# Normalised rows copied by DMA into one-pass-type tiles and transposed as that type

## The chip, the cores and the metric

The kernel runs on one core of a Trainium2 chip. The metric is the device time of one execution in microseconds, as the median of repeated runs. Profiles are of one execution each, taken by the hardware profiler; their times count from the span's start.

## What is computed

A two-layer encoder in float32 runs over two requests, of 512 and 256 tokens, with shared weights. Width is 1024, the hidden width of the feed-forward blocks 2816. Each layer is

```
x = x + 0.5 * FFN(rmsnorm(x, g0))
x = x + Mixer(rmsnorm(x, g1))
x = x + 0.5 * FFN(rmsnorm(x, g2))

rmsnorm(x, g) = x * rsqrt(mean(x*x) + 1e-6) * g
FFN(h) = (silu(gate) * up) @ w2,   gate, up = split(h @ w1)
```

The mixer of layer 0 is a gated linear recurrence in both directions (HGRN2); that of layer 1 is attention in a window of 128 tokens to each side, with partial rotation and sinks. A last rmsnorm ends it. So there are six normalisations that feed a matmul: before f0, before HGRN, before f1, before f2, before attention, before f3 (f0 to f3 are the four FFNs). The code numbers them by `row`, 0 to 5.

## The kernel before, in words

**Tokens and halves.** The 768 tokens are six blocks of 128 rows, b0 to b5. x lives in SBUF as six tiles of 128 x 1024 with tokens on the partitions. Blocks 0 to 2 are half 0, blocks 3 to 5 half 1; each half has 384 tokens (`H`, `HB = 3`).

**Precision.** Matmuls are float32 products made of three passes of a one-pass type, `float32r`. Every operand is split into a high part (a cast to float32r, on ACT, L166, L199, L265) and a low part (the difference, on DVE, L167, L200, L266), and `mm3` (L258 to L262) issues high x high, high x low, low x high. The FFN's wide products use the seven products of Strassen's scheme (`up_pair` L436, `down_quad` L500).

**Normalising and transposing.** A matmul needs its activations with features on the partitions. When the last contribution to a block of x has been added (L520, L522), `norm_block` runs: ACT squares the row and sums it (L310), ACT takes the root (L311), DVE the reciprocal (L312), and DVE multiplies x by it into a new tile `xn` (L313). `turn(half, part, row)` then transposes on TensorE: for each of four groups of 128 features it makes three transposes, one for each block of the half, side by side in one PSUM tile (L330), and ACT moves the tile out with the gain g as its scale (L341, or L344 with DVE's low part L345 in front of a mixer; L337 and L338 in the first one). A turn of half 0, part 0 makes features 0 to 511 for b0, b1, b2. Per row that is 2 halves x 2 parts x 4 groups x 3 blocks = 48 transposes, 288 in all. They are issued as plain float32, with the identity read as float32.

In attention, tiles that are float32r already are transposed as that type by `transpose_r` (L931), and its probabilities as float32 (L1167).

**Order.** Everything is traced in program order, and a planner then orders each engine's instructions by their readiness as it expects it, with program order as the priority; semaphores enforce the dependences. Within one engine instructions run strictly in the order so written. `later` and `run_later` put the turns off: a block's end calls `after_block` (L381), which queues the two turns of a half when its third block is done; `run_later` runs one queued step after b4, one after b5, and the rest among the first matmuls of the next stage. So, in program order, half 0's turns stand behind the matmuls of b4 and of b5 and half 1's among the first products of the next FFN (`up_plain`) or the first projection of the mixer (`proj_tok`).

**Queues.** Weights are loaded by DMAs issued from SP (L151, L185) and combined by accumulating DMAs from GpSimd (L141). ACT issues the DMAs that spill x around each mixer (L591) and bring it back (L597), and the small tables. A DMA issue that waits for a semaphore stands in its engine's order like any other instruction.

**Tiles.** `big` is a pool of 21 slots of 128 x 6 KB. `xn`, the transposed operands (14 in use through an FFN) and the hidden activations come from it.

The change touches `load_x` (L282 to L285), `norm_block` (L304) and `turn` (L317), and adds two helpers.

Of the kernel before, what the change touches and what calls it, by code (L numbers as in the profile page):

```python
# [9 lines left out]
F32 = mybir.dt.float32  # L10
F32R = mybir.dt.float32r
# [5 lines left out]
P = 128  # L17
# [18 lines left out]
HB = H // P  # L36
# [11 lines left out]
class Trunk:  # L48
# [219 lines left out]
    def load_x(self, srcs):  # L268
        nc = self.nc
        self.x = [None] * NBLK  # L270
        last = None
        blocks = [srcs[s][lo : lo + P, :] for s, (_, n) in enumerate(SEQS) for lo in range(0, n, P)]
        for b, src in enumerate(blocks):
            self.x[b] = self.xt()
            with self.tc.issue_after(last) if last else nullcontext():
                last = nc.sync.dma_start(self.x[b], src).ins
            if b == HB - 1:
                with self.tc.issue_after(last):
                    self.load_next()
                    self.load_next()  # L280
                last = self.last_load.ins
        order = None  # L282
        for b in range(HB):
            with self.tc.issue_after(order) if order else nullcontext():
                order = self.norm_block(b, vector=b == 1) or order  # L285
        self.turn(0, 0, 0, True)
        self.turn(0, 1, 0, True)
        with self.tc.issue_after(order):
            self.stage_next()
            self.stage_next()  # L290
        self.load_tables()

        def rest():
            for b in range(HB, NBLK):
                self.norm_block(b)
            for part in range(2):
                for kp in range(2):
                    self.block(part, 0, 0)
                    o = self.ops[(f"b{part}0", kp)].bitcast(F32)
                    nc.vector.tensor_add(self.tn[(part, 0)][:, kp], o[:, :, 0, :], o[:, :, 1, :])  # L300

        self.later(rest, lambda: self.turn(1, 0, 0), lambda: self.turn(1, 1, 0), self.sums)

    def norm_block(self, b, vector=False):  # L304
        nc = self.nc
        xn, r = self.big([P, D]), self.stat(1)
        if vector:
            nc.vector.tensor_tensor_reduce(xn, self.x[b], self.x[b], 1.0, 0.0, ALU.mult, ALU.add, r)
        else:
            nc.scalar.activation(xn, self.x[b], AF.Square, accum_out=r)  # L310
        last = nc.scalar.activation(r, r, AF.Sqrt, bias=self.eps, scale=1.0 / D).ins  # L311
        nc.vector.reciprocal(r, r)  # L312
        nc.vector.tensor_scalar(xn, self.x[b], r, None, ALU.mult)  # L313
        self.xn[b] = xn
        return last

    def turn(self, half, part, row, first=False):  # L317
        nc = self.nc
        feeds_ffn = row % 3 != 1
        if half == 0 and part == 0:  # L320
            if feeds_ffn:
                self.ops = {}
                self.tn = {}
            else:
                self.h = [self.big([P, 2, T], F32R) for _ in range(NC)]
        for m in range(4 * part, 4 * part + 4):
            pt = self.ps(H)
            for i in range(HB):
                src = self.xn[HB * half + i][:, m * P : (m + 1) * P]
                nc.tensor.transpose(pt[:, i * P : (i + 1) * P], src, self.ident)  # L330
            g = self.cols[:, row * NC + m : row * NC + m + 1]
            if first:
                name, kp = f"b{part}{half}", m % 4 // 2
                if (name, kp) not in self.ops:
                    self.ops[(name, kp)] = self.big([P, 2, 2, H], F32R)
                hi, lo = self.operand(name, m % 4)
                nc.scalar.activation(hi, pt, AF.Copy, scale=g)  # L337
                nc.vector.scalar_tensor_tensor(lo, pt, g, hi.bitcast(F32), ALU.mult, ALU.subtract)  # L338
                continue
            if feeds_ffn:  # L340
                nc.scalar.activation(self.block(part, half, m % 4), pt, AF.Copy, scale=g)  # L341
                continue
            hi, lo = (self.h[m][:, i, half * H : (half + 1) * H] for i in range(2))
            nc.scalar.activation(hi, pt, AF.Copy, scale=g)  # L344
            nc.vector.scalar_tensor_tensor(lo, pt, g, hi.bitcast(F32), ALU.mult, ALU.subtract)  # L345
        if feeds_ffn and not first:
            for kp in range(2):
                self.put(f"b{part}{half}", kp, self.tn[(part, half)][:, kp])
# [30 lines left out]
    xn = [None] * NBLK  # L379
# [925 lines left out]
```

## Time and profile before

| | |
|---|---|
| median of 3 runs | 2813.54 us (2812.93 to 2815.74) |
| span of the profiled execution | 2810.8 us |
| TensorE busy | 2781.0 us, 99% |
| TensorE weight loads | 2557.5 us, 91% |
| DVE busy | 2171.4 us, 77% |
| ACT busy | 1321.2 us, 47% |
| GpSimd busy | 372.5 us, 13% |
| granted TensorE clock, mean | 0.999 |
| moved by DMA | 291.37 MB, mean 104 GB/s |

The profiled execution's own time is its span, 2.7 us below the median of the runs.

How to read the rows: L330 is line 330 of the kernel. PE is TensorE's matmul (transposes too), PEld its weight load, DVE VectorE, ACT ScalarE, POOL GpSimd, SP SyncE; a name with q is that engine's sequencer. In a timeline a row is: start in us, duration in us, engine, line, operation, out<-in by the names of tiles, shapes, xcount of merged instructions, and in brackets the idle time before it and what ended it. In the groups of instructions, behind the bar, stand total busy us and the mean ns of one, then the idle time before. Matmuls are pipelined: the duration of one (0.27 us for a transposition) is longer than the distance from one to the next, and the distance is what a stream of them costs. The chain is followed back from the last instruction to what released each step; only what is on it sets the end.

### The profile page before, as it was taken

Reading aid. Unit: us, or ns where it says so; the run is one execution under the profiler, and the core shown is the slowest. Engines: PE = TensorE matmul, PEld = TensorE weight load, DVE = VectorE, ACT = ScalarE, POOL = GpSimd, SP = SyncE. Lnnn points to the kernel's source line nnn. Section 1 sums busy time; section 2 is a strip of 40 time slices with the busy share of each in tenths; the row PEclk is TensorE's granted clock in tenths of the full one; section 3 lists DMA queues with packets and bytes.
Section 4 is the critical chain, followed back from the end, with each engine's and each line's share of the span. In section 5 each row is a group of like instructions: output and inputs, shape, how many; then the busy total and the mean of one; then the engine's idle time right before and its main releaser. Section 6 shows DMA issues by size and latency. Waiting matters only on the chain.

```text
span 2810.8 us, 40561 instructions
## 1 busy us (share of the span) xinstructions
PE 2781.0 (99%) x15225; PEld 2557.5 (91%) x15225; DVE 2171.4 (77%) x3760; ACT 1321.2 (47%) x2447; POOL 372.5 (13%) x402
## 2 busy tenths in 40 slices
PE   8999999999999999999999999999999899999998
PEld 8999999889899889999999999999888789999998
DVE  8788788477577558878878887887848878878877
ACT  7444444434344336444444644444457756444443
POOL 2111120000000001111111111111102211211110
PEclk9999999999999999999999999999999999999999
DMA  6554464311111133555454355545422013555543
GB/s 174 127 128 120 113 147 123 106 44 38 46 38 38 61 98 76 136 132 126 117 129 120 76 142 132 124 116 124 135 72 76 33 50 83 143 134 125 119 114 108
DMA packets 330100, 291.37 MB, mean 104 GB/s; under 512 B 11608, under 2 KB 257840, under 8 KB 329904
## 3 DMA queue, kind: packets, MB, share of 16 engines
q1 hardware_dynamic: 293920, 212.37, 26.0%
q0 software_dynamic: 31680, 62.93, 13.0%
q10 hardware_dynamic: 4304, 13.49, 1.4%
q8 instruction: 119, 1.95, 0.3%
q14 instruction: 77, 0.63, 0.1%
HBM read 216.39 MB, written 9.44 MB: 80 GB/s over the span
## 4 chain that ended last, share of the span: by engine, by line
PE 95%; ACT 2%; DVE 2%; POOL 0%; issue 0%; DMA 0%; ACTq 0%; DVEq 0%; POOLq 0%
PE ps L436 41%; PE ps L500 20%; PE ps L262 8%; PE ps L260 8%; PE ps L261 8%; PE ps L692 3%; PE ps L786 1%; PE ps L330 1%; PE ps L762 1%; ACT big L1145 1%; PE ps L1167 1%; POOL big L1161 0%; PE ps L1129 0%; PE ps L931 0%; DVE x L522 0%
## 5 line engine op out<-in xcount | busy, mean ns | idle before, releaser
L436 PE MATMUL ps<-big,w 128*128 128x384 f32 x6720 | 1169.3, 334 | 0.0
L436 PEld LDWEIGHTS ps<-big,w 128*128 128x128 f32 x6720 | 1165.9, 188 | 1.7 <-ACT tA L453 0.2
L199 ACT CAST w<-wr 128x512 fp32r<-128x512 f32 x600 | 416.2, 707 | 687.2 <-PE ps L436 277.8
L500 PE MATMUL ps<-w,big 128*128 128x512 f32 x2520 | 575.3, 389 | 0.0
L500 PEld LDWEIGHTS ps<-w,big 128*128 128x128 f32 x2520 | 472.7, 188 | 97.5
L200 DVE TENSOR_TENSOR w<-wr,w 128x512 fp32r<-128x512 f32 (+1 forms) x520 | 434.7, 840 | 146.6 <-ACT w L199 130.8
L522 DVE SCALAR_TENSOR_TENSOR x<-ps,x 128x512 f32<-128x512 f32 x468 | 301.8, 682 | 10.0 <-PE ps L262 9.9
L141 POOL DMA_DIRECT2D s<-wr x120 | 105.9, 882 | 1511.1 <-DMA wr<-in_ffn_w_dram 643.0
L260 PE MATMUL ps<-w,big 128*128 128x512 f32 x624 | 249.3, 400 | 0.3
L262 PE MATMUL ps<-w,big 128*128 128x512 f32 x624 | 244.8, 392 | 2.1 <-DVE big L1005 1.1
L261 PE MATMUL ps<-w,big 128*128 128x512 f32 x624 | 244.0, 391 | 0.0
L260 PE MATMUL ps<-big,w 128*128 128x384 f32 (+2 forms) x640 | 220.4, 346 | 0.5 <-ACT w L166 0.4
L261 PE MATMUL ps<-big,w 128*128 128x384 f32 (+2 forms) x640 | 216.2, 338 | 0.2
L262 PE MATMUL ps<-big,w 128*128 128x384 f32 (+2 forms) x640 | 215.3, 336 | 0.0
L265 ACT CAST big<-tA 128x384 fp32r<-128x384 f32 x296 | 148.0, 513 | 114.0 <-DVE tA L475 36.2
L167 DVE TENSOR_TENSOR w<-wr,w 128x1024 fp32r<-128x1024 f32 x92 | 111.8, 1221 | 83.9 <-ACT w L166 78.5
L266 DVE TENSOR_TENSOR big<-tA,big 128x384 fp32r<-128x384 f32 x296 | 164.7, 567 | 6.7 <-ACT big L265 4.5
L200 POOL TENSOR_TENSOR w<-wr,w 128x512 fp32r<-128x512 f32 x80 | 135.4, 1692 | 202.6 <-ACT w L199 202.6
L166 ACT CAST w<-wr 128x1024 fp32r<-128x1024 f32 x92 | 96.6, 1052 | 122.2 <-PE ps L261 100.6
L206 DVE TENSOR_TENSOR wr<-wr,wr 128x512 f32<-128x512 f32 (+1 forms) x120 | 127.1, 1059 | 21.8 <-issue 20.8
L262 PEld LDWEIGHTS ps<-w,big 128*128 128x128 f32 x624 | 117.1, 188 | 28.5 <-DVE big L1005 1.9
L141 POOL DMA_DIRECT2D wr<-wr x100 | 88.1, 881 | 405.0 <-DVE w L200 166.5
(174 smaller groups left out, 3279.1 us busy)
## 6 DMA issues: line engine op xcount, KB each, us to landing
wr<-in_ffn_w_dram SPq DMA_DIRECT2D x264, 512.0 KB, 4.0
s<-in_ffn_w_dram SPq DMA_DIRECT2D x120, 256.0 KB, 3.2
s<-wr POOLq DMA_DIRECT2D x120, 256.0 KB, 4.9
wr<-wr POOLq DMA_DIRECT2D x80, 256.0 KB, 3.8
wr<-in_hg_w_in_dram SPq DMA_DIRECT2D x40, 512.0 KB, 3.8
wr<-wr POOLq DMA_DIRECT2D x20, 512.0 KB, 4.6
spill<-x ACTq DMA_DIRECT2D x12, 512.0 KB, 3.1
x<-spill ACTq DMA_DIRECT2D x12, 512.0 KB, 3.3
```

Of the source, the lines that this page charges most:

```text
L141: self.nc.gpsimd.dma_start(out, src, accum_op=ALU.add)
L199: nc.scalar.copy(h, src)
L200: (eng or nc.vector).tensor_sub(l, src, h.bitcast(F32))
L206: add = {"second": lambda: nc.vector.tensor_add(a11, a11, a21), "fourth": lambda: nc.vector.tensor_add(a12, a12, a11)}
L260: nc.tensor.matmul(out, a[0], b[0], start=first, stop=False)
L261: nc.tensor.matmul(out, a[0], b[1], start=False, stop=False)
L262: nc.tensor.matmul(out, a[1], b[0], start=False, stop=last)
L265: self.nc.scalar.copy(hi, src)
L266: self.nc.vector.tensor_sub(lo, src, hi.bitcast(F32))
L436: self.nc.tensor.matmul(ps, a[x], b[y], start=first and k == 0 and i == 0, stop=k == 3 and i == 2, skip_group_check=True,)
L500: nc.tensor.matmul(ps, a[x], w[y], start=name == chain and kp == 0 and q == 0, stop=kp == 1 and q == 2, skip_group_check=True,)
L522: self.nc.vector.scalar_tensor_tensor(x, ps, c, x, ALU.mult, ALU.add)
```

## The change

Outside the first half of the first normalisation, the normalised rows of the first two blocks of each half (b0, b1, b3, b4) are copied, byte for byte, by a DMA that ACT issues, into a new tile declared float32r, and the transposes of these blocks are issued in that type with the float32r identity (`transpose_r`). The third block of each half (b2, b5) is transposed as float32 as before. DMA writes the bits unchanged, where a cast to float32r would round them.

```diff
-                order = self.norm_block(b, vector=b == 1) or order
+                order = self.norm_block(b, vector=b == 1, first=True) or order
...
-    def norm_block(self, b, vector=False):
+    def norm_block(self, b, vector=False, first=False):
...
         nc.vector.tensor_scalar(xn, self.x[b], r, None, ALU.mult)
-        self.xn[b] = xn
+        self.xn[b] = xn if first or b % HB == HB - 1 else self.raw_copy(xn)
         return last
+
+    def raw_copy(self, src):
+        t = self.big(src.shape, F32R)
+        self.nc.scalar.dma_start(t.bitcast(F32), src)
+        return t
+
+    def turn_over(self, dst, src):
+        if src.dtype == F32R:
+            self.transpose_r(dst, src)
+        else:
+            self.nc.tensor.transpose(dst, src, self.ident)
...
-                nc.tensor.transpose(pt[:, i * P : (i + 1) * P], src, self.ident)
+                self.turn_over(pt[:, i * P : (i + 1) * P], src)
```

In numbers: 22 copies of 512 KB (two before f0, four before each of the other five), and 176 of the 288 transposes in the other type. Nothing else is changed.

## The prediction

> **What bounds the kernel now.** I read the page first (busy shares, then the chain that ended last), then that chain in order of time at the six places where L330 transposes, then the timelines of PE, DVE and ACT there.
>
> ```profile
> span 2810.8 us, 40561 instructions
> ...
> PE 2781.0 (99%) x15225; PEld 2557.5 (91%) x15225; DVE 2171.4 (77%) x3760; ACT 1321.2 (47%) x2447; POOL 372.5 (13%) x402
> ...
> PE 95%; ACT 2%; DVE 2%; POOL 0%; issue 0%; DMA 0%; ACTq 0%; DVEq 0%; POOLq 0%
> ...
> L330 PE MATMUL ps<-ident_r,big 128*128 128x128 f32 x288 | 41.0, 285 | 1.2 <-DVE big L313 1.2
> ```
>
> TensorE is busy 99% of the span and holds 95% of the chain, so at first sight each nanosecond taken from a transposition is a nanosecond of the kernel. The last row limits the prize: the L330 transposes are 288 instructions and 41 us of busy time. The 24 of half 0 at the start are left as they are; of the other 264 two in three change type, 176.
>
> Whether a saved nanosecond counts is a matter of the stage. The chain by line, and a few of its pieces in order of time (start, us, what):
>
> ```profile
> by line: PE ps L436 41.5%; PE ps L500 20.4%; PE ps L262 8.3%; PE ps L260 8.3%; PE ps L261 8.3%; PE ps L692 3.3%; PE ps L786 0.9%; PE ps L330 0.6%; PE ps L762 0.6%; ACT big L1145 0.5%; PE ps L1167 0.5%; POOL big L1161 0.4%; PE ps L1129 0.3%;
> ...
> 8.86 2.63 PE ps L330 x11
> ...
> 499.64 1.31 PE ps L330 x12
> ...
> 1540.18 1.32 DVE big L313 x2
> ...
> 1542.90 1.15 ACT big L310 x2
> ...
> 1544.70 1.41 ACT big L341 x3
> ...
> 2052.32 0.63 PE ps L931 x8
> ```
>
> L330 has 0.6% of the chain: 0.006 x 2810.8 = 16.9 us. The 2.63 us at 8.86 are unchanged ones. That leaves 14.3 us, at 1.31 / 12 = 109 ns each about 130 of the 264 on the chain. Around the others the chain runs through DVE and ACT: in the stage between the first two FFNs that follow each other (1540 to 1546), through the normalising multiply L313, the squares L310 and the evictions L341. A faster transposition there frees nobody.
>
> **What a transposition saves.** The chain rows give 109 ns for a float32 one and 0.63 / 8 = 79 ns for one of the one-pass type (L931, attention). The changed groups are mixed, two of the new type and then one old, and for that the nearest rows are those where attention has both side by side:
>
> ```profile
> 2143.75 0.46 PE L931 MATMUL ps<-ident_r,big 128*128 128x128 f32 x4
> 2144.05 0.62 PE L1167 MATMUL ps<-ident_r,big 128*128 128x128 f32 x4
> ...
> 2230.82 0.54 PE L931 MATMUL ps<-ident_r,big 128*128 128x128 f32 x4
> 2231.19 0.62 PE L1167 MATMUL ps<-ident_r,big 128*128 128x128 f32 x4
> ```
>
> Start to start, four take 0.30 us behind matmuls (75 ns each) and 0.37 us right behind float32 ones (93 ns each). So one saves 16 to 34 ns; I take 25. On the chain, 130 x 2/3 = 87 of them: **2.2 us** (1.4 to 3.0). If all 176 counted: 4.4 us (2.8 to 6.0).
>
> A rule speaks against this. The Trainium skill, "TensorE: Matmul & The Clock Gate", section "LDWEIGHTS (loading the stationary operand)", has a weight load cost columns / 1.2 ns, an estimate of 107 ns here for either type, since each transposition loads a new stationary block. By it 109 ns could fall by 2 and the saving would be about nothing; the 75 to 79 ns above say that loads follow each other faster than that, but no row shows the exact mixture.
>
> **What the copies add.** There are 22 (b3 and b4 for the first FFN, then four per stage for five stages), each 512 KB, from SBUF to SBUF, issued by ACT behind the DVE multiply. No such copy is in the trace. The nearest rows are the spills, also 512 KB and also issued by ACT:
>
> ```profile
> L591 ACTq DMA_DIRECT2D spill<-x x12: 326/333/1642, 491.0 to 2046.2; - x12
> ...
> DMA to landing us min/median/max: 2.6/3.1/5.8
> ```
>
> I take 3.1 us from issue to landing, with 2.6 and 5.8 as ends. A block used to be ready when L313 ended; now it is ready 3.1 us later. Is there room? For half 0 the late one is b1 (b0 is earlier and b2 isn't copied). Its L313 and the first transposes, for the stages before the HGRN mixer, f2, attention, and f1:
>
> ```profile
> 497.75 0.75 DVE L313 TENSOR_SCALAR big<-x,stat 128x1024 f32<-128x1024 f32 x1
> ...
> 499.47 1.48 PE L330 MATMUL ps<-ident_r,big 128*128 128x128 f32 x12
> ...
> 1540.10 1.41 DVE L313 TENSOR_SCALAR big<-x,stat 128x1024 f32<-128x1024 f32 x2
> ...
> 1541.98 1.47 PE L330 MATMUL ps<-ident_r,big 128*128 128x128 f32 x12
> ...
> 2030.21 0.75 DVE L313 TENSOR_SCALAR big<-x,stat 128x1024 f32<-128x1024 f32 x1
> ...
> 2031.94 0.27 PE L330 MATMUL ps<-ident_r,big 128*128 128x128 f32 x1
> ...
> 1046.52 0.75 DVE L313 TENSOR_SCALAR big<-x,stat 128x1024 f32<-128x1024 f32 x1
> ...
> 1052.05 0.49 PE L330 MATMUL ps<-ident_r,big 128*128 128x128 f32 x3
> ```
>
> Before the HGRN mixer b1 is ready at 498.50, its copy at 501.6, the transposes begin at 499.47: **2.1 us late**. Before f2: 1540.80 + 3.1 = 1543.9 against 1541.98, 1.9 late. Before attention: 2030.96 + 3.1 = 2034.1 against 2031.94, 2.1 late. Before f1, where blocks come out of the output projection, 1047.27 + 3.1 = 1050.4 against 1052.05: in time, by 1.7. The stage before f3 has the same shape as f1's. So three stages out of five have a copy that is late by about 2 us, 1.4 at the short end (2.6 us, before f2) and 4.8 at the long end (5.8 us).
>
> What happens then depends on the order in which PE's instructions were written. That this order follows readiness and not the program shows where half 1 is transposed:
>
> ```profile
> 508.20 0.71 PE L330 MATMUL ps<-ident_r,big 128*128 128x128 f32 x5
> 508.67 0.48 PE L261 MATMUL ps<-w,big 128*128 128x512 f32 x1
> 508.98 0.27 PE L330 MATMUL ps<-ident_r,big 128*128 128x128 f32 x1
> ```
>
> The program issues the transposes of half 1 three by three, b3, b4, b5. Here they come five, then singly between matmuls of the projection: each was set where its block was expected. I therefore expect b5's twelve matmuls to be moved ahead of b1's transposes. At the spacing of
>
> ```profile
> 1543.52 0.40 PE L261 MATMUL ps<-w,big 128*128 128x512 f32 x1
> 1543.75 0.40 PE L262 MATMUL ps<-w,big 128*128 128x512 f32 x1
> ```
>
> 0.23 us they last 2.8 us, which covers the 2 us. It isn't free before f2, where the chain goes on through ACT's evictions:
>
> ```profile
> 1542.90 1.06 ACT L310 ACTIVATE big<-x 128x1024 f32<-128x1024 f32 x1 [1.21 <-DVE x L522]
> ...
> 1543.96 0.56 ACT L341 ACTIVATE big<-ps,cols 128x384 f32<-128x384 f32 x1
> ```
>
> The first eviction needs all three blocks of a tile. With b1 landing at 1543.9, a transposition and its 0.27 us behind it, it starts at about 1544.4 and not 1543.96: **0.4 us**. Before the two mixers the chain runs on through DVE, and b5's additions (L522), which come 1.3 us earlier when PE takes b5 first, are what it follows; I charge **0.3 us** for each, with 0 and 2 as ends.
>
> For half 1, b3 and b4 have more room. Before f2 the rows are:
>
> ```profile
> 1545.44 0.76 DVE L313 TENSOR_SCALAR big<-x,stat 128x1024 f32<-128x1024 f32 x1
> ...
> 1547.73 0.60 PE L330 MATMUL ps<-ident_r,big 128*128 128x128 f32 x4
> ```
>
> The multiply is b4's; its copy is there at 1549.3. The four transposes are b3's alone, b4's come later, among the matmuls of the first projection. I cost half 1 at nothing; those matmuls are its cover, and without them each late copy would cost its lateness.
>
> **At the start** there is less room:
>
> ```profile
> 19.75 1.41 DVE L313 TENSOR_SCALAR big<-x,stat 128x1024 f32<-128x1024 f32 x2
> ...
> 22.29 1.04 PE L330 MATMUL ps<-ident_r,big 128*128 128x128 f32 x8
> ...
> 24.23 0.44 PE L260 MATMUL ps<-big,w 128*128 128x384 f32 x1 [0.39 <-ACT w L166]
> ...
> 21.65 1.28 ACT L311 ACT_TABLE_LOAD   x1
> ```
>
> The eight transposes at 22.29 fill time in which PE would wait for ACT's cast (it still waits at 24.23). Their copies land at about 24.2, so they move to where PE is the bound: 8 x 85 ns = **0.7 us**. If ACT's order shifts here, a table load more or less is 1.3 us; so 0 to 2.
>
> **On ACT** a DMA issue waits for its L313 and everything behind it on ACT (squares, casts, evictions) waits too, at most L312 and L313, about 0.9 us. ACT idles before squares for longer than that (1.21 us in the row above), and issues that do not wait cost it nothing visible. I charge **0.5 us** over the kernel; the ends are 0 and 3. The Trainium skill, "Perfetto Trace Analysis", section "DMA Instruction — HWDGE (DVE, Sync)", puts such a wait in the sequencer, so that nothing behind it is even queued; no row here has a waiting issue on ACT. DVE gets no work. The copies are 22 x 0.52 = 11.5 MB, and the two extra tiles per half come when the FFN's 14 operand tiles are free: nothing for either, and if a weight load is pushed back by a copy, up to the copy's 3.1 us, its staging has slack in these stages.
>
> **Sum:** -2.2 + 0.4 + 0.6 + 0.7 + 0.5 = 0.0 us. The profiled span stays 2810.8 and the median, 2.7 us above it, stays at **2813.5**. A measurement of this kernel can tell about 0.2%, 5.6 us, from no change.
>
> **The rivals.**
> *The order keeps b1's transposes in front* (slower). PE then stands still until the copy lands: 1.9 us before f2, and before the two mixers, where spills sit in the same ACT queue, between 2.1 (landing 3.1) and 4.8 (landing 5.8), say 3.5 each. 8.9 - 2.2 + 0.7 + 0.5 = +7.9: **2821.5**, from 2818 to 2824. For it: the expected landing by which the order is written need not be the real one. Against it: the scattered transposes above. It decides once PE's wait in front of L330 exceeds about 2.5 us per stage.
> *Everything counts* (faster). The DVE and ACT chains have slack that the chain view hides, all 176 save 34 ns and the order costs nothing: -6.0, **2807.5**. Against it: the pieces at 1540 to 1546, which hold no PE.
> *The new type isn't quicker in this mixture*, because the weight load sets the pace at 109 ns for both: 0 + 2.2 of costs, **2815.7**. Against it: 75 to 93 ns next to float32 ones. The LDWEIGHTS rule above would have it so.
>
> **Chances.** Forecast 0.53, order kept 0.30, everything counts 0.12, not quicker 0.05. Faster by over 0.2%: 0.10 (most of the third); slower by over 0.2%: 0.25 (most of the second, a little of the first); the rest, 0.65, within. The range, 2807.0 to 2823.0, holds the forecast, the fourth case, half of the third and most of the second.
>
> **What would show it.** Right: L330 split into about 176 and 112, the former 75 to 93 ns apart; copies landing 2.6 to 3.5 us after issue; before f2 and the mixers b5's L260 to L262 standing ahead of b1's transposes; PE's wait in front of L330 under 1 us per stage. Wrong: PE waits of 2 us and more on a copy; ACT idle behind its own DMA issues by over 3 us in all; a change in the FFN loops (52 to 480 and the like), which I expect to be equal to the microsecond.

## The result and the profile after

The change made the kernel slower: **2863.66 us** (2861.92 to 2864.51, 4 runs) against 2814.58 us (2812.93 to 2815.74, the three runs above and a fourth), a ratio of 1.0178 (1.0166 to 1.019). The forecast was 2813.5 with a range up to 2823.0. The profiled execution has a span of 2861.5 us, 50.7 more than that of before. In the kernel after, the multiply is still L313; the copy is L319, the float32 transposes L326, those of the one-pass type L942 (attention's 144 among them), the evictions L352 and L355 with the low part L356, the additions to x L531 and L533.

The page of the kernel after, its span, busy times and chain:

```profile
span 2861.5 us, 40606 instructions
...
PE 2791.4 (98%) x15225; PEld 2564.9 (90%) x15225; DVE 2165.9 (76%) x3760; ACT 1326.4 (46%) x2449; POOL 370.1 (13%) x402
...
PE 93%; DVE 3%; ACT 3%; DMA 1%; issue 0%; POOL 0%; ACTq 0%; DVEq 0%; POOLq 0%
```

TensorE stands idle for 2861.5 - 2791.4 = 70.1 us, against 2810.8 - 2781.0 = 29.8 before: **40.3 of the 50.7 us are new idle time**. The other 10.4 are busy time, though 176 transposes became cheaper. What TensorE waited for (total us, times, longest):

```profile
PE ps L260 <- ACT big L265: 19.2, 3, 7.3
PE ps L260 <- DVE big L356: 12.6, 2, 6.3
...
PE ps L942 <- DMA big<-big: 4.3, 4, 3.0
PE ps L326 <- DVE big L313: 3.5, 3, 1.8
```

The two large rows are five waits of about 6 to 7 us, one in each of the five stages between two blocks of the network, and TensorE waits there for the operands of the next stage: the split (L265) of an eviction in front of an FFN, the low part (L356) in front of a mixer. For the copies themselves it waits 4.3 us, 3.0 of them in one wait at the start. The same view for ScalarE:

```profile
ACT big L310 <- DVE big L313: 23.8, 14, 2.6
...
ACT big L352 <- DVE big L313: 7.5, 3, 2.6
...
ACT big L355 <- DVE big L313: 4.9, 2, 2.5
```

None of the three is in the kernel before. A square does not read what L313 writes, nor does an eviction read the L313 named here; between them and L313 stands a copy's issue. 23.8 + 7.5 + 4.9 = **36.2 us** of ScalarE. The timeline in front of the HGRN mixer shows it, first before (the idle time and what ended it are in the brackets):

```profile
491.02 1.06 ACT L310 ACTIVATE big<-x 128x1024 f32<-128x1024 f32 x1 [0.28 <-DVE x L522]
...
493.69 1.04 ACT L310 ACTIVATE big<-x 128x1024 f32<-128x1024 f32 x1
...
494.95 1.06 ACT L310 ACTIVATE big<-x 128x1024 f32<-128x1024 f32 x1
...
497.67 1.06 ACT L310 ACTIVATE big<-x 128x1024 f32<-128x1024 f32 x1 [1.20 <-DVE x L522]
...
500.59 1.06 ACT L310 ACTIVATE big<-x 128x1024 f32<-128x1024 f32 x1 [1.44 <-DVE x L522]
...
501.65 0.56 ACT L344 ACTIVATE big<-ps,cols 128x384 fp32r<-128x384 f32 x1
```

and after:

```profile
500.76 1.06 ACT L310 ACTIVATE big<-x 128x1024 f32<-128x1024 f32 x1 [0.28 <-DVE x L533]
...
505.55 0.48 ACTq L319 DMA_DIRECT2D big<-big  x1
506.08 1.07 ACT L310 ACTIVATE big<-x 128x1024 f32<-128x1024 f32 x1 [2.56 <-DVE big L313]
...
510.99 0.47 ACTq L319 DMA_DIRECT2D big<-big  x1
511.51 1.06 ACT L310 ACTIVATE big<-x 128x1024 f32<-128x1024 f32 x1 [3.96 <-DMA spill<-x]
...
515.77 0.47 ACTq L319 DMA_DIRECT2D big<-big  x1
516.29 1.06 ACT L310 ACTIVATE big<-x 128x1024 f32<-128x1024 f32 x1 [1.27 <-DVE big L313]
...
520.52 0.47 ACTq L319 DMA_DIRECT2D big<-big  x1
521.04 2.00 ACT L355 ACTIVATE big<-ps,cols 128x384 fp32r<-128x384 f32 x4 [2.47 <-DVE big L313]
```

Before, the squares follow the arrival of the blocks, 1 to 3 us apart. After, each copied block goes through square, root, reciprocal, multiply and issue before the next square starts, 5.3 and 5.4 us apart for the first two. (The 3.96 us in front of the square at 511.51 are put down to a spill, but that square too starts 0.52 us behind the start of a copy's issue; the 36.2 us don't hold this wait.) From the first square to the first eviction it was 501.65 - 491.02 = 10.6 us; now it is 521.04 - 500.76 = **20.3 us**. That is the number to follow through the experiments. It stands for one transition of five: it tells the ends of the range apart, but it doesn't rank the runs between (13.2 and 15.4 us go with nearly the same time).

**The second price is the clock.** Windows of the kernel after around the wait in front of f1 (from:to, length, busy time of PE, PEld, DVE, ACT, POOL with instructions, granted clock, DMA share, GB/s):

```profile
1074.00:1080.00 6.00, 0.11 (x1) 0.00 (x0) 3.41 (x6) 3.35 (x8) 0.87 (x1) 0.67 0.92 279
1080.00:1085.50 5.50, 5.42 (x17) 5.14 (x18) 4.31 (x6) 5.48 (x12) 0.86 (x1) 0.50 0.57 110
1085.50:1095.00 9.50, 9.50 (x65) 9.40 (x64) 3.25 (x5) 6.86 (x13) 0.00 (x0) 0.96 0.00 0
```

TensorE does nothing for 6 us, and for the 5.5 us that follow it runs at a clock of 0.50: 17 instructions in 5.42 us of busy time, where the next window has 65 instructions in 9.50. So this wait of 6 us costs some 2.7 us more (half of 5.5), and that is booked as busy time. In the 10 us behind each of the five waits the mean clock was 0.79, 0.69, 0.76, 0.81 and 0.78, so some 4 to 6 us of each ran at half, an estimate of 11.7 us lost in all. With 2.8 us at the start (below) that is 14.5 us, about what busy time lost: it rose by 10.4 us, though the transposes became some 4.6 us cheaper (the run with the new type alone, below). The Trainium skill, "TensorE: Matmul & The Clock Gate", section "Part 1: The HAM clock gate", has the clock fall to half after an idle window of about 3.4 us and come back after as long a busy one; this trace agrees in kind, with 6 us idle and about 5.5 us at half, but the wait of 3.01 us at the start was followed by half the clock too. The mean granted clock of the span fell from 0.999 to 0.990.

What did not change: the FFN loops. The same stretch of 336 matmuls after and before, from the chains in order of time:

```profile
119.11 58.26 PE ps L447 x336
```

```profile
109.38 58.26 PE ps L436 x336
```

It starts 119.11 - 109.38 = 9.7 us later: a fifth of the 50.7 us is lost ahead of it, around the first normalisation, and the rest between there and the start of f3's loop.

### The profile page after: what moved, and what is told of

It reads as the page before. It is cut to its first block, busy times and chain, and to the rows that moved or that the text cites. A ratio compares the mean times of both kernels' runs of the same rounds, so it can differ in the third digit from the quotient of the medians.

```text
span 2861.5 us, 40606 instructions
## 1 busy us (share of the span) xinstructions
PE 2791.4 (98%) x15225; PEld 2564.9 (90%) x15225; DVE 2165.9 (76%) x3760; ACT 1326.4 (46%) x2449; POOL 370.1 (13%) x402
## 3 DMA queue, kind: packets, MB, share of 16 engines
q0 software_dynamic: 31680, 62.93, 13.2%
## 4 chain that ended last, share of the span: by engine, by line
PE 93%; DVE 3%; ACT 3%; DMA 1%; issue 0%; POOL 0%; ACTq 0%; DVEq 0%; POOLq 0%
PE ps L447 40%; PE ps L511 20%; PE ps L260 8%; PE ps L261 8%; PE ps L262 8%; PE ps L703 3%; PE ps L797 1%; PE ps L942 1%; PE ps L773 1%; PE ps L1178 1%; ACT big L1156 0%; DVE w L167 0%; PE ps L1140 0%; DVE big L313 0%; PE ps L1191 0%
## 5 line engine op out<-in xcount | busy, mean ns | idle before, releaser
L447 PEld LDWEIGHTS ps<-big,w 128*128 128x128 f32 x6720 | 1165.9, 188 | 2.2 <-DVE tA L473 0.6
L511 PEld LDWEIGHTS ps<-w,big 128*128 128x128 f32 x2520 | 472.5, 188 | 100.1 <-ACT big L265 2.5
L533 DVE SCALAR_TENSOR_TENSOR x<-ps,x 128x512 f32<-128x512 f32 x468 | 302.3, 685 | 12.1 <-PE ps L262 12.1
L260 PE MATMUL ps<-big,w 128*128 128x384 f32 (+2 forms) x640 | 224.4, 352 | 19.2 <-ACT big L265 19.2
L261 PE MATMUL ps<-big,w 128*128 128x384 f32 (+2 forms) x640 | 219.7, 344 | 0.0
L262 PE MATMUL ps<-big,w 128*128 128x384 f32 (+2 forms) x640 | 218.1, 341 | 0.0
L265 ACT CAST big<-tA 128x384 fp32r<-128x384 f32 x296 | 148.7, 516 | 118.0 <-DVE tA L479 38.0
L260 PEld LDWEIGHTS ps<-w,big 128*128 128x128 f32 x624 | 118.8, 190 | 35.1 <-DVE big L356 13.1
L260 PEld LDWEIGHTS ps<-big,w 128*128 128x128 f32 x640 | 123.9, 194 | 26.3 <-ACT big L265 19.8
L262 PEld LDWEIGHTS ps<-w,big 128*128 128x128 f32 x624 | 118.3, 190 | 26.9 <-DVE big L1016 1.9
```

Of the source, the lines that this page charges most:

```text
L260: nc.tensor.matmul(out, a[0], b[0], start=first, stop=False)
L261: nc.tensor.matmul(out, a[0], b[1], start=False, stop=False)
L262: nc.tensor.matmul(out, a[1], b[0], start=False, stop=last)
L265: self.nc.scalar.copy(hi, src)
L447: self.nc.tensor.matmul(ps, a[x], b[y], start=first and k == 0 and i == 0, stop=k == 3 and i == 2, skip_group_check=True,)
L511: nc.tensor.matmul(ps, a[x], w[y], start=name == chain and kp == 0 and q == 0, stop=kp == 1 and q == 2, skip_group_check=True,)
```

## The experiments

The kernel before took 2813.08, 2812.61, 2812.74, 2813.18 and 2812.89 us beside the five groups of runs; ratios are to those, with 95% intervals. "Lag" is the time from the first square to the first eviction in front of the HGRN mixer.

| run | median us | ratio | lag us |
|---|---|---|---|
| before | 2814.58 | | 10.6 |
| after | 2863.66 | 1.0178 (1.0166 to 1.019) | 20.3 |
| copies unread | 2860.96 | 1.017 (1.0155 to 1.0186) | 20.3 |
| copies of x | 2821.77 | 1.0031 (1.002 to 1.0042) | 10.9 |
| copies by GpSimd | 2839.02 | 1.0091 (1.0076 to 1.0106) | 15.7 |
| rounded, second tile | 2832.75 | 1.0068 (1.0053 to 1.0083) | 14.5 |
| second tile alone | 2830.23 | 1.0064 (1.0049 to 1.0079) | 14.6 |
| rounded, one tile | 2811.87 | 0.9998 (0.9988 to 1.0007) | 10.6 |
| copy behind next square | 2831.68 | 1.0067 (1.0052 to 1.0082) | 13.2 |
| copies of b0, b1 | 2831.51 | 1.0063 (1.0048 to 1.0078) | 15.4 |
| copies of b3, b4 | 2853.41 | 1.0144 (1.0129 to 1.0159) | 17.0 |
| second tile early | 2814.32 | 1.0005 (0.9996 to 1.0014) | 10.7 |
| copies, tile early | 2828.84 | 1.0059 (1.0047 to 1.0072) | 11.7 |

**First theories.** A: ScalarE, whose instructions run in order, stands behind each copy's issue while that waits for L313. B: the transposes wait for the copies to land. C: the new order of TensorE's instructions, or the new type, costs.

*Copies that nobody reads.*

```diff
-        self.xn[b] = xn if first or b % HB == HB - 1 else self.raw_copy(xn)
+        self.xn[b] = xn
+        if not first and b % HB < HB - 1:
+            self.raw_copy(xn)
```

> The 22 copies are issued by ACT as in the change, but nothing reads them: all transposes read the float32 rows. Theory A (ACT's in-order queue stands behind each copy's issue, which waits for DVE's L313, and the evictions and casts behind it are late): slow nearly as the change, 2845 to 2865 us, with ACT idle for 2 us and more behind single issues. Theory B (the transposes wait for the copy to land, 3.3 us after issue): nothing waits for a copy any more, so 2812 to 2818 us. Theory C (the planner's new order of PE's instructions is itself bad): 2812 to 2820 us, since PE's instructions have the old operands.

2860.96 us. All but 2.7 us of the loss is there with float32 transposes that wait for no copy, and the waits of TensorE are those of the change:

```profile
PE ps L260 <- ACT big L265: 19.0, 3, 7.2
PE ps L260 <- DVE big L358: 12.6, 2, 6.3
```

So B and C don't have the bulk.

*Copies of x in place of the normalised rows* (the issue doesn't wait for L313; what is transposed is then x itself, without the normalisation).

```diff
-        self.xn[b] = xn if first or b % HB == HB - 1 else self.raw_copy(xn)
+        self.xn[b] = xn if first or b % HB == HB - 1 else self.raw_copy(self.x[b])
```

> The copies read x, which is long complete for ACT when its squares are done, and not the normalised rows; so the transposed rows are not normalised. Size, queue, landing and type of the transposes stay, the wait for L313 goes. Theory A: most of the 49 us come back, 2810 to 2822 us. Theory B: the copies start about 1 to 2 us earlier and the transposes still wait for them, 2840 to 2860 us. Theory C: the order is like that of the change, 2850 to 2865 us.

2821.77 us: 41.9 of the 49 us are gone with the wait for L313, though copies, landings and new type are all there. At this point A looked settled.

*Copies issued by GpSimd.*

```diff
-        self.nc.scalar.dma_start(t.bitcast(F32), src)
+        self.nc.gpsimd.dma_start(t.bitcast(F32), src)
```

> The copies are issued by GpSimd and not by ACT; GpSimd is busy 13% of the span. Theory A: ACT has no waiting issue, so 2808 to 2822 us; what is left shows how much the late landing costs. Theory B: landing is no earlier (the 512 KB accumulating copies of GpSimd took 4.6 us), so 2855 to 2875 us. Theory C: 2850 to 2865 us.

2839.02 us. ScalarE has no copy to wait behind, and half of the loss stays. TensorE's wait for copies is larger here, from this kernel's waits:

```profile
PE ps L942 <- DMA big<-big: 12.9, 7, 4.0
```

That explains a part, but the lag is still 15.7 us.

*No copies: L313 writes rounded rows into a second tile of the one-pass type.*

```diff
-        nc.vector.tensor_scalar(xn, self.x[b], r, None, ALU.mult)
-        self.xn[b] = xn if first or b % HB == HB - 1 else self.raw_copy(xn)
+        if first or b % HB == HB - 1:
+            nc.vector.tensor_scalar(xn, self.x[b], r, None, ALU.mult)
+        else:
+            xn = self.big([P, D], F32R)
+            nc.vector.tensor_scalar(xn, self.x[b], r, None, ALU.mult)
+        self.xn[b] = xn
```

> No copies at all: DVE's L313 writes its result directly into a float32r tile for the same blocks, which rounds these rows, and 176 transposes run in that type. This measures what the other type is worth alone. My estimate on record: 2.2 us on the chain, up to 6.0 if all count, so 2808 to 2813 us. All theories expect the same; if the mixture isn't quicker, 2814 to 2815 us.

2832.75 us, the surprise: no DMA, no wait of ScalarE, and yet 19.7 us. A is not enough. What this kernel shares with the change is the new type and the second tile.

*The second tile without the new type, and the new type without a second tile*, to tell theory S (the second tile costs) from theory T (the new type disturbs).

```diff
+        if not (first or b % HB == HB - 1):
+            xn = self.big([P, D])
         nc.vector.tensor_scalar(xn, self.x[b], r, None, ALU.mult)
-        self.xn[b] = xn if first or b % HB == HB - 1 else self.raw_copy(xn)
+        self.xn[b] = xn
```

> No copies and no new type: the only thing left of the change is its second tile per copied block (Square writes into one tile, L313 writes the normalised rows into another, both plain float32). The rounded kernel, which has the second tile and the new type but no copies, lost 18 to 20 us. Theory S (the second tile, taken from a pool of 21, makes squares or allocations late): 2828 to 2836, as much as the rounded kernel and 2 more for the slower transposition. Theory T (the new type itself disturbs): 2811 to 2816. Theory A alone (everything comes from the queue behind the copies): 2811 to 2816 too, so a time near before would leave T for the rounded kernel.

```diff
-        xn, r = self.big([P, D]), self.stat(1)
+        xn, r = self.big([P, D], F32 if first or b % HB == HB - 1 else F32R), self.stat(1)
...
-        self.xn[b] = xn if first or b % HB == HB - 1 else self.raw_copy(xn)
+        self.xn[b] = xn
```

> The new type with no second tile and no copy: the tile of a copied block is a one-pass tile from the start, Square writes its scratch into it and L313 overwrites it with the rounded rows (so the low bits are lost, the transposes are of the new type). Theory S: nothing is left but the quicker transposes, 2808 to 2813 (the sum of the prediction had -2.2 us for them). Theory T: 2828 to 2836, as the rounded kernel with its second tile.

2830.23 and 2811.87 us. The second tile alone costs **17.6 us**; its first square and its first eviction in front of the HGRN mixer are 14.6 us apart:

```profile
495.14 1.06 ACT L310 ACTIVATE big<-x 128x1024 f32<-128x1024 f32 x1 [0.28 <-DVE x L535]
...
509.70 1.96 ACT L357 ACTIVATE big<-ps,cols 128x384 fp32r<-128x384 f32 x4
```

The new type alone can't be told from nothing. The page of the kernel with the type alone:

```profile
span 2810.2 us, 40565 instructions
...
PE 2776.4 (99%) x15225; PEld 2552.0 (91%) x15225; DVE 2166.3 (77%) x3760; ACT 1321.6 (47%) x2447; POOL 375.3 (13%) x402
```

Busy time fell by 2781.0 - 2776.4 = 4.6 us, 26 ns for each of the 176 transposes, and idle time rose from 29.8 to 33.8: what the transposes save is given back as waiting.

*Each copy behind the next block's square; copies of one half only.*

```diff
-            nc.scalar.activation(xn, self.x[b], AF.Square, accum_out=r)
+            square = nc.scalar.activation(xn, self.x[b], AF.Square, accum_out=r).ins
+            if self.uncopied:
+                was, src = self.uncopied.pop()
+                with self.tc.issue_after(square):
+                    self.xn[was] = self.raw_copy(src)
...
-        self.xn[b] = xn if first or b % HB == HB - 1 else self.raw_copy(xn)
+        self.xn[b] = xn
+        if not first and b % HB < HB - 1:
+            self.uncopied.append((b, xn))
```

> All copies, issued by ScalarE, but each one ordered behind the Square of the next block, by when L313 of its own block has had about as long as a Square takes. Theory A (ACT stands behind an issue that waits for L313): the wait shrinks from 2.6 us to under 1, and what remains is the second tile's price: 2820 to 2838. Theory B (the transposes wait for the landing): the copies land later still, 2863 or more. If it is still 2855 or more with short waits of ACT, neither has the cause.

2831.68 us: with the squares freed, 32 us come back and about 19 stay, about as much as the second tile alone costs.

```diff
-        self.xn[b] = xn if first or b % HB == HB - 1 else self.raw_copy(xn)
+        self.xn[b] = xn if first or b % HB == HB - 1 or b > HB - 1 else self.raw_copy(xn)
```

> Copies of blocks 0 and 1 only; blocks 3 and 4 stay plain float32. The prediction held that the second half costs nothing, so that all of the loss would sit in the first half: then 2855 to 2866. If blocks 3 and 4 have a share (their squares and multiplications stand in ACT's and DVE's queues behind the copies of blocks 0 and 1, ahead of f1, attention and HGRN), the loss falls with the number of issues: half of 49 us, 2835 to 2842.

The other half, `b < HB` in that place:

> Copies of blocks 3 and 4 only. The prediction charged the second half at nothing: 2811 to 2816. With the first half alone at 2831.5 and the whole at 2863.7, what is left for the second half, if the two add, is 31 us: 2838 to 2848. In between: the halves do not add, the loss being made where both crowd the same queue and pool.

2831.51 and 2853.41 us. The second half alone costs 40.7 us, twice the first half's 18.9, and the two do not add up to the whole: neither forecast of the second half held.

**Why a tile costs time.** Theory S: a second tile of the pool of 21 crowds it. Rival O: the planner writes another order as soon as the square and L313 don't share a tile. Two tests of S:

```diff
-SLOTS = 21
+SLOTS = 20
```

> The kernel before with nothing changed but the pool: 20 slots in place of 21. Theory S: the pool is short at the transitions, so one slot less costs there too, some 3 to 20 us: 2816 to 2833. Rival O: the number of slots does not matter, 2811 to 2815.

```diff
-        xn, r = self.big([P, D]), self.stat(1)
+        own = first or b % HB == HB - 1
+        xn = self.big([P, D]) if own else self.tp.tile([P, D], mybir.dt.bfloat16, tag="tA", name=self.name("tA"), bufs=8)
+        r = self.stat(1)
...
+        if not own:
+            xn = self.big([P, D])
         nc.vector.tensor_scalar(xn, self.x[b], r, None, ALU.mult)
...
```

> No copies, no new type. As the kernel with the second plain tile per copied block (2830), but Square writes its scratch as bfloat16 into a 2 KB tile of another pool (tA), and the only tile of the pool of 21 is the one that L313 writes. Theory S (the second tile's slot in the pool of 21 is what costs 18 us): 2809 to 2816. Rival O (the planner orders the block otherwise as soon as Square and L313 don't share a tile, slots or not): 2826 to 2834.

One slot less, in the kernel before, costs 4.7 us (2817.46, ratio 1.0017, 1.0007 to 1.0026). With the square's scratch out of the pool, a block holds one tile as before, and still 13.8 of the 17.6 us stay (2826.5, 1.0049, 1.0034 to 1.0064). S falls. The two remedies together, scratch elsewhere and copies behind the next square:

```diff
+        xn = self.big([P, D]) if own else self.tp.tile([P, D], mybir.dt.bfloat16, tag="tA", name=self.name("tA"), bufs=8)
...
+                with self.tc.issue_after(square):
+                    self.xn[was] = self.raw_copy(src)
...
```

> All copies, with both suspects taken down: each copy is issued by ScalarE behind the Square of the next block (no wait for L313), and Square's scratch is a bfloat16 tile of another pool, so that a copied block holds no tile of the pool of 21 before L313 and two only from L313 to the landing of its copy. If A and S are the whole cause: 2812 to 2822, the upper end if two tiles for some 5 us still crowd the pool or if b1's and b4's copies land late. If it stays at 2828 or more, a part of the late copies' 2831.7 has another cause (the landing, or the second tile after L313).

2831.26 us (1.0068, 1.0051 to 1.0085): nothing gained over the late copies alone.

**Theory P**, from the order in which ScalarE's instructions are written: a tile of the pool is handed out in program order of first writers. An instruction that takes a new tile can't be placed ahead of one that stands earlier in the program and takes a tile too. In the kernel before the first writer of a block's tile is the square, which is ready early. If L313 (or the copy) takes a tile, then everything behind it in program order that takes one is planned behind it: the next block's square, and in front of a mixer the evictions, whose eight `h` tiles come from the same pool. First test, again without copies, no square of a later block takes such a tile (the lines show the difference to the run at 2826.5):

```diff
-        own = first or b % HB == HB - 1
+        own = first
```

> No copies, no new type. As the run with the scratch in a tile of tA (2826.5), but now for all three blocks of a half, the uncopied one too. Theory P: the planner hands out the 21 tiles in program order of their first writers, so a Square that writes such a tile cannot be placed ahead of L313 of the block before if that L313 takes a new tile; this delays the squares in ScalarE's order. Here no Square takes a tile of that pool, and in the order as built the three squares of the start stand again as in the kernel before: 2810 to 2817. Rival S (the count of tiles held) is met as well; rival O (any tile of its own for L313 disturbs) says 2824 to 2830 as before.

2829.31 us (1.0055, 1.004 to 1.007): no gain, so P as I had applied it, to the squares alone, failed. Its first square and its first eviction in front of the HGRN mixer:

```profile
495.67 1.06 ACT L312 ACTIVATE tA<-x 128x1024 bf16<-128x1024 f32 x1 [0.28 <-DVE x L537]
...
510.62 0.56 ACT L359 ACTIVATE big<-ps,cols 128x384 fp32r<-128x384 f32 x1
```

15.0 us of lag, though the first five squares stand as far apart as in the kernel before. What is late are the evictions: in ScalarE's order they now stand behind b5's square. That fits P, since every L313 takes its tile late here and, in program order, L313 of b4 stands ahead of them; the planner's reason itself isn't in the trace. Three more runs of that group have copies and small scratch for all blocks. The late copies with it:

```diff
+        xn = self.big([P, D]) if first else self.tp.tile([P, D], mybir.dt.bfloat16, tag="tA", name=self.name("tA"), bufs=8)
...
+                with self.tc.issue_after(square):
+                    self.xn[was] = self.raw_copy(src)
...
```

> All copies, each behind the Square of the next block, and Square's scratch of all blocks in tiles of tA. Theory P: nothing orders a Square behind a copy or behind L313 any more; what is left is the issues themselves (0.5 us of ScalarE each) and the landing, as in the run that copied x (2821.8, which had neither wait): 2815 to 2826. If P is wrong about the squares, 2828 to 2834 as with scratch of the copied blocks alone.

The changed kernel with the scratch alone:

```diff
+        xn = self.big([P, D]) if first else self.tp.tile([P, D], mybir.dt.bfloat16, tag="tA", name=self.name("tA"), bufs=8)
...
+        if not first:
+            xn = self.big([P, D])
         nc.vector.tensor_scalar(xn, self.x[b], r, None, ALU.mult)
```

> All copies where the change has them, with no order forced; the one edit to the changed kernel is Square's scratch in tA for all blocks, so that L313 takes the tile of the normalised rows. Theory P: the planner is free to place the next Square ahead of the copy and does so in the order as built, at the start and in front of attention; in front of the HGRN mixer b3's and b4's copies still stand ahead of four evictions. Most of the 49 us is gone with one edit that touches neither the copies nor the transposes: 2816 to 2832. If the wait for L313 at the issue is the cause whatever the order of the squares (theory A as first put): 2845 or more.

And that with GpSimd's issues:

```diff
-        self.nc.scalar.dma_start(t.bitcast(F32), src)
+        self.nc.gpsimd.dma_start(t.bitcast(F32), src)
```

> As the run before in this call, with the copies issued by GpSimd in place of ScalarE. ScalarE then has no issue to stand behind; the transposes still wait for the landing. Theory P with landing and issues as the rest: 2814 to 2824, below the run with ScalarE's issues by what those cost. If it is at 2830 or more, the landing is dearer than the run with GpSimd's copies and the shared tile (2839.0) had it (its landing waits came to 12.9 us).

They took 2836.57 (1.0082, 1.0067 to 1.0097), 2838.38 (1.0089, 1.0072 to 1.0106) and 2840.61 us (1.0099, 1.0084 to 1.0114): 23 to 27 us back, the rest not, and all three above what I expected of them.

The last pair takes the tile's slot early instead: GpSimd writes one column of the tile ahead of the square, and nothing else moves.

```diff
         xn, r = self.big([P, D]), self.stat(1)
+        if not (first or b % HB == HB - 1):
+            own = self.big([P, D])
+            nc.gpsimd.memset(own[:, :1], 0.0)
...
+        if not (first or b % HB == HB - 1):
+            xn = own
         nc.vector.tensor_scalar(xn, self.x[b], r, None, ALU.mult)
```

> No copies, no new type: the second plain tile per copied block, as in the run at 2830.2, but GpSimd writes one column of it ahead of the Square, so that the tile gets its slot as early as the Square's own. Theory P (tiles of the pool are handed out in program order of their first writers; whatever takes a tile behind L313 in program order, the next Square or the evictions of a mixer's turn, is planned behind L313): the order of ScalarE in front of the HGRN mixer is that of the kernel before again, and the time too: 2810 to 2819, the upper part if the slot that is held longer costs as much as one slot less (+4.7). If a second tile disturbs by anything but the order: 2826 to 2832.

2814.32 us, +1.4, and the lag is 10.7 us again:

```profile
491.68 1.06 ACT L313 ACTIVATE big<-x 128x1024 f32<-128x1024 f32 x1 [0.28 <-DVE x L538]
...
502.37 0.56 ACT L360 ACTIVATE big<-ps,cols 128x384 fp32r<-128x384 f32 x1
```

(In this kernel L313 is the square.) GpSimd's four writes for this stage stand at 468 to 475 us in the trace, long ahead of the first square. A block holds its second tile for longer than in the run at 2830.23, and the loss can't be told from nothing: **it is the order, not the tile.** The same early write for the tile that the copy fills, in the changed kernel:

```diff
+            own = self.big([P, D], F32R)
+            nc.gpsimd.memset(own.bitcast(F32)[:, :1], 0.0)
...
-        self.xn[b] = xn if first or b % HB == HB - 1 else self.raw_copy(xn)
+        self.xn[b] = xn if first or b % HB == HB - 1 else self.raw_copy(xn, own)
...
```

> The changed kernel, all copies issued by ScalarE, with the one-pass tile's slot taken early by the same one-column write ahead of the Square. Theory P: the squares stand ahead of the copies and the first evictions ahead of some; what is left is the issue (0.5 us each), the landing and the slots held longer: 2816 to 2830. If ScalarE's wait at the issue costs whatever the order of squares and evictions: 2845 to 2864. Freeing the squares by small scratch left 2838.4, since L313 then took the tile late; P says this run is below that one.

2828.84 us: one column written early takes back **34.8 of the 49 us** (2863.66 - 2814.58), with every copy issued by ScalarE as before. Its squares and evictions (L313 and L357 here), TensorE's waits, and ScalarE's waits for the multiply (L316 here):

```profile
495.82 1.06 ACT L313 ACTIVATE big<-x 128x1024 f32<-128x1024 f32 x1 [0.28 <-DVE x L535]
...
507.54 1.06 ACT L357 ACTIVATE big<-ps,cols 128x384 fp32r<-128x384 f32 x2 [0.82 <-PE ps L328]
```

```profile
PE ps L944 <- DMA big<-big: 5.5, 3, 3.9
PE ps L261 <- DVE big L266: 4.6, 5, 2.3
...
PE ps L260 <- ACT big L265: 3.1, 2, 2.7
```

```profile
ACT big L265 <- DVE big L316: 4.7, 3, 2.4
...
ACT stat L314 <- DVE big L316: 2.8, 2, 1.4
```

The issues wait for the multiply as before, but less work stands behind them: ScalarE's idle time behind it is 4.7 + 2.8 = 7.5 us, against 36.2. No wait of TensorE on these operands exceeds 3.9 us any more, and the mean clock is back at 0.998. The 16 us that stay (over the 2812.89 us of that group) are idle time: 2826.0 - 2780.0 = 46.0 us against 29.8. A part is the landing of the copies: at the start TensorE waits 3.9 us for the first one, and the stretch of 336 matmuls begins at 114.18, 4.8 us later than in the kernel before; how the rest divides among issues, splits and slots held longer was not taken apart. No version beat the kernel before.

The planner's rule is inferred, from the order of ScalarE's instructions and from these times; that the moment at which the tile is taken decides is what the last pair shows. With P the early runs can be read differently, though no run shows that by itself. The copies of x may have lost little not only because their issue doesn't wait, but also because their tile is taken at once, since x is ready: lag 10.9. And P explains why the copies that nobody reads hurt as much as the others: the tile is handed out late in both.

## Why the prediction was wrong, point by point

**The step that failed** is the one on ScalarE: "I charge 0.5 us over the kernel; the ends are 0 and 3". I had the right queue and the wrong order in it. I assumed that the copies would be put where their issue finds L313 done, and that behind a waiting issue there are "at most L312 and L313, about 0.9 us". In the profile ScalarE is idle for 36.2 us behind L313, because the copy is placed ahead of the next square: the waiting time is the whole round through root, reciprocal and multiply, 2.6 us at the longest of one wait, and each block's work starts only when the block before is done. The issue itself isn't free either: "issues that do not wait cost it nothing visible" stands beside a row of spills with 333 ns each, and a copy's issue took 0.47 us, some 10 us of ScalarE for 22. The prediction's own test, "ACT idle behind its own DMA issues by over 3 us in all", is met twelve times over. The Trainium skill, "Perfetto Trace Analysis", section "DMA Instruction — HWDGE (DVE, Sync)", which I cited for the wait that sits in the sequencer, was the better guide: the rows at 505.55 and 506.08, on ScalarE, are such a wait with a square standing behind it that needed nothing from it.

**"The two extra tiles per half ... nothing for either"** failed for the same reason. I asked whether the pool has room (it has: one slot less costs 4.7 us) and not when the tile is handed out. Taking it late costs 17.6 us even without a copy (2830.23), taking it early 1.4, within its interval (2814.32).

**Half 1 "at nothing"**: copies of b3 and b4 alone cost 40.7 us. The matmuls that I named as cover hide a late transposition; they don't hide a late eviction, and the evictions of half 0 stand behind the work of b3 and b4 in the program.

**The start**, 0.7 us with an end at 2: the kernel after is 9.7 us late by f0's stretch of 336 matmuls (119.11 against 109.38). In the first 50 us TensorE's busy time fell by 41.12 - 36.28 = 4.8 us and the granted clock to 0.93, from the windows of before and after:

```profile
0.00:50.00 50.00, 41.12 (x234) 40.12 (x235) 42.71 (x65) 38.23 (x64) 10.43 (x10) 1.00 0.70 187
```

```profile
0.00:50.00 50.00, 36.28 (x192) 34.76 (x193) 32.78 (x52) 33.16 (x54) 4.84 (x9) 0.93 0.72 202
```

The first copy, issued at 19.64, takes 6.0 us to land, and TensorE waits for it:

```profile
25.77 0.72 PE L942 MATMUL ps<-ident_r,big 128*128 128x128 f32 x4 [3.01 <-DMA big<-big]
```

From 25.77 to 31.40 the granted clock was 0.50, which costs 2.8 us more.

**The clock** isn't in the prediction. Neither the waits of 6 to 7 us nor the half-rate stretch behind each of them were foreseen.

**Saving per transposition**: right in size, 26 ns measured against 25 taken (16 to 34). Wrong in what it is worth: -2.2 us was forecast for the 87 on the chain, and the type alone gave -0.7, with an interval that holds zero. The rival by which the new type would not be quicker named a saving of nothing, which the type alone can't be told from, but by luck: its reason, 109 ns for both types, doesn't hold.

**Landing**, 3.1 us (2.6 to 5.8), over all copies and for the two at the start:

```profile
DMA to landing us min/median/max: 2.9/3.3/8.4
```

```profile
DMA to landing us min/median/max: 6.0/7.2/8.4
```

Right for the other 20, which landed after 2.9 to 5.3 us, and too short for the two at the start, where weights are being loaded. The waits are 4.3 us in all; the longest, 3.0 us at the start, is above the 2 us that I had named as a sign of error and has the half-rate stretch behind it.

**The order on TensorE**: right. In front of f2 b0's first four transposes are followed by twelve matmuls of the down projection, b5's by their place, and only then come the others:

```profile
1566.58 0.46 PE L942 MATMUL ps<-ident_r,big 128*128 128x128 f32 x4
1566.88 0.47 PE L260 MATMUL ps<-w,big 128*128 128x512 f32 x1
...
1569.70 1.32 PE L942 MATMUL ps<-ident_r,big 128*128 128x128 f32 x12
...
1579.90 0.69 PE L260 MATMUL ps<-big,w 128*128 128x384 f32 x1 [7.29 <-ACT big L265]
```

```profile
1577.13 2.00 ACT L352 ACTIVATE big<-ps,cols 128x384 f32<-128x384 f32 x4 [2.25 <-DVE big L313]
```

The row of 1579.90 is the wait that nobody had in the sum: the last transposition is over at 1579.90 - 7.29 = 1572.6 and TensorE stands until 1579.90, for ScalarE, whose first evictions start only at 1577.13, behind the issue of b4's copy. The slower rival (b1's transposes kept in front) had the sign and not the mechanism. **The FFN loops** are equal, as forecast, but for a wait of 1.7 us in the first stretch of f0 (at 94.37).

## What to carry to other kernels

When a step gets a new tile, ask which instruction writes it first and how late that is: under a planner that hands out a pool's tiles in program order, as this one seems to, everything behind it that takes a tile of the same pool is planned behind it, however much room there is. Look for the lag on the engines that prepare the next operands (here from square to eviction, 10.6 to 20.3 us), not on the one that is 99% busy. A DMA issued by a compute engine is an instruction in that engine's order; follow which work will stand behind it, and price the round trip it waits for, not the last step of it.

## What the runs showed of the hardware

A 512 KB copy from SBUF to SBUF issued by ScalarE landed after 2.9 us at the least and 3.3 in the median, like a spill, but the two issued in the first 26 us, while the core's DMA moved some 300 GB/s (the window from 20 to 30 us), took 6.0 and 8.4 us. An issue keeps ScalarE itself for 0.47 us in the median: behind it the next instruction starts about 0.5 us after the issue's own start (505.55 and 506.08, 515.77 and 516.29).

Each of the five waits of TensorE of 6 to 7 us was followed by some 4 to 6 us at half the clock, so its price is over a third more than the wait (11.7 us on 31.8). A shorter wait can do it too: 3.01 us at 25.77 was followed by 5.6 us at 0.50, while behind the 1.79 us at 36.54 the clock stayed at 1.00. The mean over the span hides such stretches: in the last run it was 0.998, though in the 8 us behind its wait of 3.9 us the clock was 0.79.
